# Gating the next branch during the current one, and wider buffers, in the merge of a two-layer hybrid diffusion block

## Chip, cores and metric

One Trainium2 chip, one core. The metric is the device time of one execution in microseconds, and the time of a kernel is the median of its runs. The engines in the rows below are TensorE (PE, with its weight loads as PEld), VectorE (DVE), ScalarE (ACT), GpSimd (POOL) and SyncE (SP), which issues nearly all transfers.

## The reference

Two layers work on 512 latent tokens and 256 context tokens of width 1024. A layer normalises its input, projects it to 10768 columns, and runs four mixers on slices of them: A global attention, W windowed attention, G a spatial gating MLP, and M a bidirectional mLSTM. The part that matters here joins the four:

```
y    = stack(branch_k * silu(gate_k))              # 4 branches, 512 wide each
proj = einsum('bnkw,kwd->bnkd', y, w_branch)       # each to 1024
g    = sigmoid(merge)                              # merge: 4 x 1024 of the input projection's columns
out  = sum_k(g_k * proj_k) @ w_out                 # then RMSNorm, gate, residual
```

The second layer computes its output for the latent tokens alone, so its merge runs on 512 tokens, the first layer's on 768. All data is float32.

## The kernel before

**Splitting.** Each matmul on full-precision operands is made of three: operands are split into a rounded high part (ScalarE) and a remainder (VectorE), and high x high, high x low and low x high are added in PSUM. Weights are split as they arrive (`start_load`, L206 to L228): a half is loaded to a raw buffer (pool "wr", three of them), ScalarE rounds it (L226), VectorE takes the remainder (L227).

**Stages of a layer.** Projections and mixers run interleaved (`interleave`, L1299), with results stored to device memory: branch outputs in `ydram`, gate values in `sgd`, the attentions' softmax divisors in `rsd` (L912), and, for the pairs of columns named `t...` in `FILL_ORDER` (L68), the sigmoid paths of the merge in `thd`. Then `merge` (L1346) and `finish` (L1437) run. The mLSTM is the last mixer; its head 3 runs into the beginning of the merge.

**The merge.** Branches come in the order A, W, M, G (0, 1, 3, 2). For each branch the gated product is built in four steps (L1356 to L1369): a step loads 128 channels of the branch's output and its gate, and for the two attentions the divisors, spread over 64 partitions each (L1364); VectorE multiplies (L1366, L1367), ScalarE rounds the product to `gh` (L1368), VectorE writes the remainder to `gl` (L1369). Then come eight columns of 128 outputs. A column either loads its saved sigmoid path (L1380) or computes it with 24 matmuls per 512 tokens (L1386, L1387), multiplies `gh` and `gl` by the branch's weights with 12 matmuls per 512 tokens, and adds the product of both to its running sum `zb[j]` (L1394 or L1403, L1406). The first `LEAD[l]` columns of the first branch use one-bank PSUM tiles ("d", three of them), a tile per 512 or 256 tokens; the others a two-bank tile ("s", two of them). During the last branch the finished sums are split for the output projection (`split_z`, L1431), the last two after the loop.

**Buffers.** Four SBUF pools matter: "big", 4 buffers of 12 KB per partition; "m", 8 of 3 KB; "v", 2 of 6 KB; and the weights'. Layer 1 before: the sums 0 to 3 lie in two "v" buffers, 4 to 7 in one "big"; `gh` and `gl` take two "big" buffers. The loads of a gating step and the saved sigmoid paths are all in "m". Attention values and the spatial branch's rows use "v" earlier in the layer.

**Order.** The kernel is written in a tile framework: each operation gets its priority from its place in the program, buffers are handed out in that order, and the framework fixes each engine's instruction order ahead of time by a simulated timeline. At run time every engine and SyncE's queue work strictly in that order. `stream` and `take` (L177 to L240) fix the order of the weights, one unit ahead. In layer 0 the units of the spatial branch are placed into the merge at four spots (`SPOTS`, L73); in layer 1 there are none. The prologue (L357 to L480) has an order written out by hand; its lines 473 and 474 place the split of the second weight unit.

Of the kernel before, what the change touches and what calls it, by code (L numbers as in the profile page):

```python
# [10 lines left out]
F32R = mybir.dt.float32r  # L11
# [10 lines left out]
NTOK = 768  # L22
SEQ = 512
# [32 lines left out]
MERGE0 = 6672  # L56

OFF = 250
RATIO = ((1.5, 1.3, 1.5), (1.2, 0.4, 1.5))
N2, N3 = 1, 1  # L60
LEAD = (2,4)
LAG = 26.0
SIDE_UNITS = ([(0, i) for i in range(8, 12)] + [(1, i) for i in range(8)], [(1, i) for i in range(8, 12)])
SIDE_FROM = (30, 10)
# [16 lines left out]
def tile_hybrid_block(ctx, tc, A, out):  # L81
    nc = tc.nc
    sy, act, dve, pool, pe = nc.sync, nc.scalar, nc.vector, nc.gpsimd, nc.tensor
# [23 lines left out]
    def BIG(shape, dt=F32):  # L107
        return bigp.tile(shape, dt, tag="big", name="big")

    def M(n=768, dt=F32):  # L110
        return mp.tile([128, n], dt, tag="m", name="m")

    def V6(shape, dt=F32):
        return vp.tile(shape, dt, tag="v", name="v")
# [22 lines left out]
    def bc(ap, shape):  # L137
        return ap.to_broadcast(shape)

    def rd(ap):  # L140
        return ap.bitcast(F32)
# [34 lines left out]
    BRANCHES = (0, 1, 3, 2)  # L176
# [138 lines left out]
    def load_gates(l, i):  # L315
        if i % 2 == 0:
            g = gate_g[l, i // 2] = M(512)
            sy.dma_start(out=g, in_=bc(gates[l][0:1, i * 256:i * 256 + 512], [128, 512]))
        if l == 0:
            gate_c[i] = XS()  # L320
            sy.dma_start(out=gate_c[i], in_=bc(gates[l][1:2, i * 256:i * 256 + 256], [128, 256]))
# [35 lines left out]
    def prologue():  # L357
# [69 lines left out]
        with tc.manual_schedule(engines={mybir.EngineType.PE, mybir.EngineType.Activation, mybir.EngineType.DVE, mybir.EngineType.SP}):  # L427
            wm = [load_mod(0)]
            for i in range(2):
                xx.append(BIG([128, 3, D]))  # L430
                for t in range(3 * i, 3 * i + 3):
                    sy.dma_start(out=xa(t), in_=A["x"][t] if t < XT else A["ctx"][t - XT])
            split0 = start_load(0)
            wm += [load_mod(i) for i in range(1, 4)]
            pm += [B()]
            sums_of(0)
            done = []
            jk = V6([128, D])
            r = squares(0)
            wm += [load_mod(i) for i in range(4, KT)]  # L440
            split1 = start_load(1)
            for t in range(NT):
                done.append(turned(t, r))
                if t + 1 < NT:
                    r = squares(t + 1)
                if t == 0:
                    rows_of(0)
                if t > 0:
                    back(t - 1, done[t - 1])
            column(0)  # L450
            warm(4)
            split0((0,))
            back(NT - 1, done[NT - 1])
            wh, wl = take(("in", 0, "a_kv"), 0)
            w = held["w"] = v3(wh[:, :8 * 272], 8), v3(wl[:, :8 * 272], 8)
            s2, s3 = S(), S()
            acc = [DB(), DB(), DB(), s2[:, 0:512], s2[:, 512:1024]]
            pm += [s3[:, 0:512], s3[:, 512:1024]]
            sums_of(1)
            channels(0)  # L460
            rows_of(1)
            warm(2)
            column(1)
            warm(4)
            split0((1,))
            for j in range(KT):
                if j + 1 < KT:
                    channels(j + 1)
                for i, (ps, t) in enumerate(zip(acc, TILES)):
                    if i == 2 and j + 2 < KT:  # L470
                        sums_of(j + 2)
                        rows_of(j + 2)
                    if i == 2 and j in (5, 6):
                        split1((j - 5,))
                    if i == 4 and j + 2 < KT:
                        column(j + 2)
                    tok_step(ps, w, 272, t, j)
# [868 lines left out]
    def merge(l, ydram, rsd, sgd, thd):  # L1346
        want_c = l == 0
        n = NTOK if want_c else SEQ
# [3 lines left out]
        zb = []  # L1352
        zs = {}
        done = False
        for bi, b in enumerate(BRANCHES):
            gh, gl = BIG([128, 4, NTOK], F32R), BIG([128, 4, NTOK], F32R)  # L1356
            for k in range(4):
                yt, sg = M(768), M(768)
                sy.dma_start(out=yt[:, :n], in_=ydram[b, k][:, :n])
                sy.dma_start(out=sg[:, :n], in_=sgd[b, k][:, :n])  # L1360
                if b < 2:
                    rs = M(768)
                    for i in range(2):
                        sy.dma_start(out=rs[64 * i:64 * i + 64, :n],  # L1364
                                     in_=bc(rsd[b, 2 * k + i:2 * k + i + 1, :], [64, n]))
                    dve.tensor_mul(sg[:, :n], sg[:, :n], rs[:, :n])  # L1366
                dve.tensor_mul(yt[:, :n], yt[:, :n], sg[:, :n])  # L1367
                act.copy(gh[:, k, :n], yt[:, :n])  # L1368
                dve.tensor_sub(gl[:, k, :n], yt[:, :n], rd(gh[:, k, :n]))  # L1369
            for j in range(KT):  # L1370
                if bi == 0 and j in (0, 2, 4):
                    zt = V6([128, 2, NTOK]) if j < 4 else BIG([128, 4, NTOK])
                    zb += [zt[:, i, :] for i in range(2 if j < 4 else 4)]
                z = zb[j]
# [29 lines left out]
                                             op0=ALU.add, op1=ALU.mult)  # L1404
                if bi > 0:
                    dve.tensor_add(z[:, :n], z[:, :n], th[:, :n])  # L1406
                if bi == 3 and j < 6:
                    if j == 0:
                        pt = BIG([128, 4, NTOK], F32R)
                        parts = [pt[:, i, :] for i in range(4)]  # L1410
                    elif j in (2, 4):
                        pt = V6([128, 2, NTOK], F32R)
                        parts = [pt[:, i, :] for i in range(2)]
                    elif j > 1:
                        parts = [M(768, F32R), M(768, F32R)]
                    zs[j] = split_z(z, parts, n)
                if bi == 3 and j >= 4:
                    load_gates(l, j - 4)
                if (bi, j) in SPOTS[l]:
                    while next(gating) is not None:  # L1420
                        pass
                    done = SPOTS[l][bi, j] == "g_u1"
                elif done and tails:
                    tails.pop(0)()
        pt = BIG([128, 4, NTOK], F32R)
        parts = [pt[:, i, :] for i in range(4)]
        for j in (6, 7):
            zs[j] = split_z(zb[j], parts, n)
        return zs

    def split_z(z, parts, n):  # L1431
        h, lo = parts.pop(0), parts.pop(0)
        act.copy(h[:, :n], z[:, :n])
        dve.tensor_sub(lo[:, :n], z[:, :n], rd(h[:, :n]))
        return h, lo
# [91 lines left out]
    for l in range(2):  # L1527
        ydram = dp.tile([4, 4, 128, NTOK], F32, name=f"yd{l}")
        sgd = dp.tile([4, 4, 128, NTOK], F32, name=f"sg{l}")
# [113 lines left out]
```

## Time and profile before

| | |
|---|---|
| runs | 2050.71, 2052.67, 2054.06 us; median 2052.67 |
| profiled execution | 2052.57 us, span 2050.8 us |
| mean granted TensorE clock | 0.993 of full |
| busy: PE / DVE / ACT / POOL | 97% / 64% / 47% / 4% |
| merge of layer 0 (first to last column's work) | about 850 to 1127 us of the span |
| merge of layer 1 | about 1851 to 2000 us of the span |

Busy times are of the whole span, which is made of stages with different limits; a stage is read by its own windows and by what its engines waited for. The clock column of a window is the mean of the granted TensorE clock, 1.00 for 2.4 GHz and 0.50 for 1.2 GHz. Matmul lines carry the number of the helper that issues them (L243), so they are told apart by their tiles: "d" and "s" are the PSUM tiles, "big" the gated product. A transfer's line is that of its issue on SyncE; the time to landing is listed by form.

### The profile page before, as it was taken

The page shows a single profiled execution, that of the slowest core. Times are in us where ns is not written, and L with a number is a line of the kernel's source. Part 1 is how long each engine was busy: PE and PEld are TensorE (multiplying, and loading weights), DVE is VectorE, ACT ScalarE, POOL GpSimd, SP SyncE. Part 2 cuts the span into 40 slices and gives each one's busy share as a digit, 9 for nine tenths or more (in the row PEclk, how much of TensorE's full clock was granted, in tenths as well). Part 3 has the DMA queues.
Part 4 walks back from the last instruction along what each step waited for, and adds up shares of the span by engine and source line. Part 5 has one row for each costly group of instructions (what it writes and reads, how often), then busy time and mean ns, then how long its engine had stood idle before and what let it go on. Part 6 is the DMA issues. An engine that isn't in the chain of part 4 may idle for free.

```text
span 2050.8 us, 34563 instructions
## 1 busy us (share of the span) xinstructions
PE 1992.4 (97%) x13216; PEld 1809.7 (88%) x13216; DVE 1316.1 (64%) x2857; ACT 972.9 (47%) x2178; POOL 75.1 (4%) x88
## 2 busy tenths in 40 slices
PE   7999999999999999899999989999999999998998
PEld 6898999899999899799988989989989898887778
DVE  5766865676656756567545588666685565545765
ACT  5655544354444553334332476555565465432333
POOL 1200100000000000001000021000000000000000
PEclk9999999999999999999999999999999999999999
DMA  7112223323333544665343342223333334547745
GB/s 292 63 55 78 93 94 114 122 94 126 116 106 111 181 140 152 207 217 168 100 151 115 130 153 93 84 82 111 119 117 113 124 104 160 156 136 224 239 144 180
DMA packets 124270, 274.96 MB, mean 134 GB/s; under 512 B 16032, under 2 KB 41288, under 8 KB 123464
## 3 DMA queue, kind: packets, MB, share of 16 engines
q1 hardware_dynamic: 123560, 272.13, 40.8%
q8 instruction: 104, 1.70, 0.4%
q14 instruction: 62, 0.51, 0.1%
q0 software_dynamic: 256, 0.54, 0.1%
q10 hardware_dynamic: 288, 0.07, 0.0%
HBM read 219.33 MB, written 53.36 MB: 133 GB/s over the span
## 4 chain that ended last, share of the span: by engine, by line
PE 85%; DMA 6%; DVE 4%; ACT 2%; issue 1%; SPq 0%; POOL 0%; DVEq 0%; ACTq 0%; POOLq 0%
PE d L243 59%; PE s L243 13%; PE b L243 7%; PE s L857 4%; DMA m<-rs 3%; DMA m<-sg 1%; PE d L576 1%; DVE m L1367 1%; ACT m L417 0%; DVE wl L227 0%; DMA big<-in_x_dram 0%; DMA sg<-st 0%; ACT wh L226 0%; DMA wr<-in_w_mod_dram 0%; DVE m L1366 0%
## 5 line engine op out<-in xcount | busy, mean ns | idle before, releaser
L243 PE MATMUL d<-xh,wh 128*128 128x512 f32 (+1 forms) x1504 | 537.1, 357 | 0.3 <-DVE yx L821 0.2
L243 PE MATMUL d<-xh,wl 128*128 128x512 f32 (+1 forms) x1504 | 535.1, 356 | 0.0
L243 PE MATMUL d<-xl,wh 128*128 128x512 f32 (+1 forms) x1504 | 533.2, 355 | 0.0
L227 DVE TENSOR_TENSOR wl<-wr,wh 128x1024 fp32r<-128x1024 f32 (+3 forms) x264 | 282.6, 1092 | 62.4 <-ACT wh L226 62.0
L226 ACT CAST wh<-wr 128x1024 fp32r<-128x1024 f32 (+3 forms) x264 | 238.4, 946 | 168.1 <-PE s L243 80.4
L243 PEld LDWEIGHTS d<-xh,wh 128*128 128x128 f32 x1504 | 284.5, 189 | 34.7 <-DVE st L685 0.3
L243 PEld LDWEIGHTS d<-xl,wh 128*128 128x128 f32 x1504 | 284.6, 189 | 34.3
L243 PEld LDWEIGHTS d<-xh,wl 128*128 128x128 f32 x1504 | 284.2, 189 | 34.6
L243 PE MATMUL d<-wh,xh 128*128 128x256 f32 (+1 forms) x976 | 282.6, 291 | 4.0 <-DVE xh L419 1.8
L243 PE MATMUL d<-wh,xl 128*128 128x256 f32 (+1 forms) x976 | 278.1, 285 | 0.6 <-DVE xl L420 0.5
L243 PE MATMUL d<-wl,xh 128*128 128x256 f32 (+1 forms) x976 | 278.1, 285 | 0.3 <-DVE wl L227 0.3
L243 PEld LDWEIGHTS d<-wh,xh 128*128 128x128 f32 x976 | 186.5, 192 | 7.9 <-issue 4.1
L243 PE MATMUL s<-big,wh 128*128 128x512 f32 x704 | 180.7, 363 | 8.0 <-DVE big L1369 6.5
L243 PEld LDWEIGHTS d<-wh,xl 128*128 128x128 f32 x976 | 186.9, 192 | 1.2 <-DVE xl L420 0.7
L243 PEld LDWEIGHTS d<-wl,xh 128*128 128x128 f32 x976 | 187.1, 192 | 0.8 <-DVE wl L227 0.5
L861 DVE TENSOR_TENSOR m<-s,m 128x768 fp32r<-128x768 f32 (+2 forms) x144 | 119.3, 837 | 94.9 <-ACT m L860 94.3
L825 ACT ACTIVATE m<-s,yx 128x768 f32<-128x768 f32 (+3 forms) x160 | 120.4, 753 | 97.7 <-DVE yx L823 47.8
L243 PEld LDWEIGHTS s<-big,wh 128*128 128x128 f32 x704 | 118.4, 193 | 30.6 <-DVE big L1369 7.7
L819 DVE TENSOR_REDUCE yx<-s 128x1 f32<-128x768 f32 (+3 forms) x160 | 122.5, 765 | 33.6 <-PE s L243 32.4
L860 ACT CAST m<-s 128x768 fp32r<-128x768 f32 (+2 forms) x144 | 100.7, 705 | 85.6 <-PE s L857 84.5
L243 PE MATMUL b<-m,v 128*128 128x256 f32 (+1 forms) x768 | 131.4, 285 | 0.9 <-ACT m L860 0.9
L243 PE MATMUL s<-big 128*128 128x256 f32 (+2 forms) x680 | 118.7, 303 | 1.2 <-ACT big L577 0.7
(340 smaller groups left out, 3056.1 us busy)
## 6 DMA issues: line engine op xcount, KB each, us to landing
wr<-in_w_in_dram SPq DMA_DIRECT2D x100, 512.0 KB, 4.4
wr<-in_w_mg_dram SPq DMA_DIRECT2D x50, 512.0 KB, 4.3
wr<-in_w_mod_dram SPq DMA_DIRECT2D x32, 512.0 KB, 4.5
wr<-in_w_out_dram SPq DMA_DIRECT2D x32, 512.0 KB, 4.4
th<-st SPq DMA_DIRECT2D x50, 256.0 KB, 2.3
wr<-in_w_bp_dram SPq DMA_DIRECT2D x50, 256.0 KB, 3.6
wr<-in_w_br_dram SPq DMA_DIRECT2D x28, 384.0 KB, 3.6
m<-th SPq DMA_DIRECT2D x26, 384.0 KB, 5.1
```

Source lines behind the costliest of these rows:

```text
L226: act.copy(wh[:, sl], raw)
L227: dve.tensor_sub(wl[:, sl], raw, rd(wh[:, sl]))
L243: pe.matmul(o, l, r, start=start, stop=stop)
L576: pe.transpose(pt[:, h * 128:(h + 1) * 128], st[:, h * 128:(h + 1) * 128].bitcast(F32R), ident_r)
L819: dve.reduce_max(out=mx, in_=ps[:, :n], axis=AX.X)
L825: act.activation(P, ps[:, :n], AF.Exp, bias=nm[:, 0:1], scale=sc, accum_out=sm)
L857: pe.transpose(pt[:, o:o + 128], P[:, cols[j]:cols[j] + 128], ident)
L860: act.copy(ph, pt[:, :n])
L861: dve.tensor_sub(pl, pt[:, :n], rd(ph))
L1367: dve.tensor_mul(yt[:, :n], yt[:, :n], sg[:, :n])
```

## The change

- The divisors of the first branch are no longer loaded into an "m" buffer per step, but for two steps at once into a "v" buffer, two of them.
- In layer 1 the running sums lie three to a "v" buffer (0 to 2, 3 to 5), and 6 and 7 in one "m" buffer each; none is in "big" any more.
- In layer 1 the gating steps of the next branch are written behind the columns 3 to 6 of the current one (`PP_FROM`), into a second pair of "big" buffers.
- In layer 1 the split sums lie in two "big" buffers, three sums each, and two "v" buffers for sums 6 and 7, whose split is now inside the loop. They lay in one "big", two "v" and four "m" buffers, and another "big" after the loop.
- `LEAD` goes from 2 and 4 to 4 and 6: two more columns of the first branch in one-bank tiles.
- In the prologue the first half of the second weight unit is split at input block 4 instead of 5.

```
--- before.py
+++ after.py
@@ -56,9 +56,10 @@
 MERGE0 = 6672
 
 OFF = 250
+PP_FROM = 3
 RATIO = ((1.5, 1.3, 1.5), (1.2, 0.4, 1.5))
 N2, N3 = 1, 1
-LEAD = (2,4)
+LEAD = (4,6)
 LAG = 26.0
 SIDE_UNITS = ([(0, i) for i in range(8, 12)] + [(1, i) for i in range(8)], [(1, i) for i in range(8, 12)])
 SIDE_FROM = (30, 10)
@@ -470,8 +471,8 @@
                     if i == 2 and j + 2 < KT:
                         sums_of(j + 2)
                         rows_of(j + 2)
-                    if i == 2 and j in (5, 6):
-                        split1((j - 5,))
+                    if i == 2 and j in (4, 6):
+                        split1((j // 2 - 2,))
                     if i == 4 and j + 2 < KT:
                         column(j + 2)
                     tok_step(ps, w, 272, t, j)
@@ -1352,23 +1353,53 @@
         zb = []
         zs = {}
         done = False
+        rss = {}
+
+        def gate_pair():
+            return BIG([128, 4, NTOK], F32R), BIG([128, 4, NTOK], F32R)
+
+        def load_rs(rs, b, k):
+            for i in range(2):
+                sy.dma_start(out=rs[64 * i:64 * i + 64, :n], in_=bc(rsd[b, 2 * k + i:2 * k + i + 1, :], [64, n]))
+
+        def gated(b, k, pair):
+
+            gh, gl = pair
+            if b == BRANCHES[0] and k % 2 == 0:
+                wide = V6([128, 2, NTOK])
+                for i in range(2):
+                    rss[k + i] = wide[:, i, :]
+                    load_rs(wide[:, i, :], b, k + i)
+            yt, sg = M(768), M(768)
+            sy.dma_start(out=yt[:, :n], in_=ydram[b, k][:, :n])
+            sy.dma_start(out=sg[:, :n], in_=sgd[b, k][:, :n])
+            if b < 2:
+                if b == BRANCHES[0]:
+                    rs = rss[k]
+                else:
+                    rs = M(768)
+                    load_rs(rs, b, k)
+                dve.tensor_mul(sg[:, :n], sg[:, :n], rs[:, :n])
+            dve.tensor_mul(yt[:, :n], yt[:, :n], sg[:, :n])
+            act.copy(gh[:, k, :n], yt[:, :n])
+            dve.tensor_sub(gl[:, k, :n], yt[:, :n], rd(gh[:, k, :n]))
+
+        nxt = None
         for bi, b in enumerate(BRANCHES):
-            gh, gl = BIG([128, 4, NTOK], F32R), BIG([128, 4, NTOK], F32R)
-            for k in range(4):
-                yt, sg = M(768), M(768)
-                sy.dma_start(out=yt[:, :n], in_=ydram[b, k][:, :n])
-                sy.dma_start(out=sg[:, :n], in_=sgd[b, k][:, :n])
-                if b < 2:
-                    rs = M(768)
-                    for i in range(2):
-                        sy.dma_start(out=rs[64 * i:64 * i + 64, :n],
-                                     in_=bc(rsd[b, 2 * k + i:2 * k + i + 1, :], [64, n]))
-                    dve.tensor_mul(sg[:, :n], sg[:, :n], rs[:, :n])
-                dve.tensor_mul(yt[:, :n], yt[:, :n], sg[:, :n])
-                act.copy(gh[:, k, :n], yt[:, :n])
-                dve.tensor_sub(gl[:, k, :n], yt[:, :n], rd(gh[:, k, :n]))
+            if nxt is None:
+                nxt = gate_pair()
+                for k in range(4):
+                    gated(b, k, nxt)
+            gh, gl = nxt
+            nxt = None
             for j in range(KT):
-                if bi == 0 and j in (0, 2, 4):
+                if bi == 0 and not want_c and j in (0, 3, 6, 7):
+                    if j < 6:
+                        zt = V6([128, 3, SEQ])
+                        zb += [zt[:, i, :] for i in range(3)]
+                    else:
+                        zb.append(M(768))
+                elif bi == 0 and want_c and j in (0, 2, 4):
                     zt = V6([128, 2, NTOK]) if j < 4 else BIG([128, 4, NTOK])
                     zb += [zt[:, i, :] for i in range(2 if j < 4 else 4)]
                 z = zb[j]
@@ -1404,7 +1435,17 @@
                                              op0=ALU.add, op1=ALU.mult)
                 if bi > 0:
                     dve.tensor_add(z[:, :n], z[:, :n], th[:, :n])
-                if bi == 3 and j < 6:
+                if bi == 3 and not want_c:
+                    if j in (0, 3):
+                        pt = BIG([128, 6, SEQ], F32R)
+                        parts = [pt[:, i, :] for i in range(6)]
+                    elif j == 6:
+                        pt = V6([128, 3, SEQ], F32R)
+                        parts = [pt[:, i, :] for i in range(3)]
+                    elif j == 7:
+                        parts.append(V6([128, 3, SEQ], F32R)[:, 0, :])
+                    zs[j] = split_z(z, parts, n)
+                elif bi == 3 and j < 6:
                     if j == 0:
                         pt = BIG([128, 4, NTOK], F32R)
                         parts = [pt[:, i, :] for i in range(4)]
@@ -1416,16 +1457,21 @@
                     zs[j] = split_z(z, parts, n)
                 if bi == 3 and j >= 4:
                     load_gates(l, j - 4)
+                if not want_c and bi < 3 and j >= PP_FROM and j < PP_FROM + 4:
+                    if nxt is None:
+                        nxt = gate_pair()
+                    gated(BRANCHES[bi + 1], j - PP_FROM, nxt)
                 if (bi, j) in SPOTS[l]:
                     while next(gating) is not None:
                         pass
                     done = SPOTS[l][bi, j] == "g_u1"
                 elif done and tails:
                     tails.pop(0)()
-        pt = BIG([128, 4, NTOK], F32R)
-        parts = [pt[:, i, :] for i in range(4)]
-        for j in (6, 7):
-            zs[j] = split_z(zb[j], parts, n)
+        if want_c:
+            pt = BIG([128, 4, NTOK], F32R)
+            parts = [pt[:, i, :] for i in range(4)]
+            for j in (6, 7):
+                zs[j] = split_z(zb[j], parts, n)
         return zs
 
     def split_z(z, parts, n):
```

## Rows read from the trace of the kernel before

**Rows 1.** The page, busy time, share of the span and instructions of each engine
```profile
PE 1992.4 (97%) x13216; PEld 1809.7 (88%) x13216; DVE 1316.1 (64%) x2857; ACT 972.9 (47%) x2178; POOL 75.1 (4%) x88
```

**Rows 2.** Who TensorE waited for, 840 to 870 us: total, times, longest
```profile
PE d L243 <- ACT big L1368: 7.2, 2, 5.2
```

**Rows 3.** The same view, 1840 to 2005 us
```profile
PE s L243 <- DVE big L1369: 4.5, 2, 2.6
PE d L243 <- ACT big L1368: 3.4, 3, 1.7
PE d L243 <- ACT wh L226: 1.7, 1, 1.7
PE s L243 <- DVE m L1403: 0.3, 1, 0.3
```

**Rows 4.** Windows: length, each engine's busy time, PE clock, DMA share, GB/s
```profile
860.00:870.00 10.00, 8.34 (x35) 7.08 (x36) 5.10 (x13) 1.00 (x2) 1.32 (x1) 0.66 0.81 254
```

**Rows 5.** The same view, in layer 1's merge
```profile
1910.00:1920.00 10.00, 10.00 (x46) 8.26 (x45) 7.87 (x13) 3.53 (x6) 0.00 (x0) 1.00 0.95 335
1920.00:1930.00 10.00, 8.17 (x29) 6.30 (x28) 7.76 (x13) 2.38 (x4) 0.00 (x0) 0.83 0.81 270
1910.00:1950.00 40.00, 37.26 (x154) 29.46 (x152) 30.17 (x48) 12.28 (x21) 0.00 (x0) 0.96 0.81 268
```

**Rows 6.** Timeline of SyncE, layer 0: start us, us, engine, line, transfer, count
```profile
811.67 0.32 SPq L1359 DMA_DIRECT2D m<-yd  x1
...
821.37 0.32 SPq L1360 DMA_DIRECT2D m<-sg  x1
...
829.51 1.16 SPq L1364 DMA_DIRECT2D m<-rs  x2
...
852.09 1.09 SPq L1364 DMA_DIRECT2D m<-rs  x2
...
870.66 0.33 SPq L1148 DMA_DIRECT2D yd<-m  x1
```

**Rows 7.** Timeline of VectorE, layer 0 (idle before and releaser in brackets)
```profile
833.61 0.96 DVE L1366 TENSOR_TENSOR m<-m 128x768 f32<-128x768 f32 x1 [1.08 <-DMA m<-rs]
834.60 0.96 DVE L1367 TENSOR_TENSOR m<-m 128x768 f32<-128x768 f32 x1
...
858.79 0.96 DVE L1366 TENSOR_TENSOR m<-m 128x768 f32<-128x768 f32 x1 [3.32 <-DMA m<-rs]
...
861.64 0.96 DVE L1369 TENSOR_TENSOR big<-m,big 128x768 fp32r<-128x768 f32 x1 [0.81 <-ACT big L1368]
```

**Rows 8.** By line, first and last start: divisor stores, layer 1's softmax, spatial stores
```profile
L912 SPq DMA_DIRECT2D rs<-xs x4: 318/331/416, 396.9 to 1729.1; - x4
...
L825 ACT ACTIVATE m<-s,yx x64: 672/850/927, 1254.3 to 1707.4; 128x768 f32<-128x768 f32 x32, 128x512 f32<-128x512 f32 x16, 128x640 f32<-128x640 f32 x16
...
L760 SPq DMA_DIRECT2D yd<-t x8: 360/371/384, 1656.8 to 1687.8; - x8
```

**Rows 9.** Transfers by form: count, KB of one, median us to landing
```profile
m<-sg SPq DMA_DIRECT2D x16, 384.0 KB, 5.2
...
m<-sg SPq DMA_DIRECT2D x16, 256.0 KB, 3.6
...
m<-th SPq DMA_DIRECT2D x24, 256.0 KB, 3.5
...
wr<-in_w_bp_dram SPq DMA_DIRECT2D x50, 256.0 KB, 3.6
```

**Rows 10.** Chain that ended last, 1900 to 1925 us: start, us, what
```profile
1904.05 7.96 PE s L243 x35
```

**Rows 11.** Timeline of VectorE, end of layer 1's second branch
```profile
1923.58 0.69 DVE L1367 TENSOR_TENSOR m<-m 128x512 f32<-128x512 f32 x1 [1.29 <-DMA m<-sg]
1924.19 1.89 DVE L1369 TENSOR_TENSOR big<-m,big 128x512 fp32r<-128x512 f32 x3
```

**Rows 12.** Timeline of SyncE, layer 1: store of the last mLSTM head
```profile
1879.82 0.49 SPq L1148 DMA_DIRECT2D yd<-m  x1
```

## Prediction

> **What bounds the kernel now.** I read the busy times first: TensorE is busy for 97% of the span [rows 1], so only time in which it stands still, or runs at half clock, can be won without taking matmuls away, and the change takes none away. Next, the list of who waited for whom on TensorE, limited to the two merges. In layer 0's merge TensorE waited 7.2 us in two pieces for ScalarE's rounding of the first branch's gated product (L1368) [rows 2]. In layer 1's merge it waited 4.5 us for the remainder of the gated product (L1369), 3.4 us for L1368, 1.7 us for a weight rounding (L226) and 0.3 us for an evacuation [rows 3]. Then the 10-us windows, for the clock. After each long stop it falls from 2.4 to 1.2 GHz: a mean of 0.66 means that (1 - 0.66) / 0.5 = 0.68 of the window, 6.8 us, ran at half rate [rows 4]; 0.83 means 3.4 us, in the window from 1920 and again in that from 1950 [rows 5]. Half rate costs half of the time in which TensorE had work.
>
> Last, the SyncE queue, for why the gated products are late. In layer 0 a value tile is requested at 811.67, its gate tile at 821.37, its divisor tile at 829.51, and the fourth divisor at 852.09 [rows 6]. All are buffers of the pool "m". That pool has 8, and I count 5 held by the last mLSTM head (two key products, the value tile, the output-gate tile and the tile that becomes its result), which is stored only at 870.66. So one step's three tiles use all three free buffers, and the next step starts when they come back: VectorE multiplies by the first divisor at 833.61 and by the fourth at 858.79, (858.79 - 833.61) / 3 = 8.4 us a step [rows 7].
>
> **The change, part by part.**
>
> *Divisors in two wide buffers.* The third tile of each of the four steps leaves pool "m". Its two transfers can go as soon as the pool "v" has room and the divisors are stored. The four stores of divisors lie between 396.9 and 1729.1, two per layer; layer 1's last softmax, which ends the use of the attention's values, starts at 1707.4, and the spatial branch, the third user of "v" there, stores its last piece at 1687.8 [rows 8]. In both layers that is long before the divisors are wanted, so I cost their loads at nothing; SyncE's spare time hides them, and without that cover they cost what they cost now. The third free "m" buffer then holds the next step's value tile. A step becomes: gate tile's load 5.2 us in layer 0 [rows 9], then two products, after which its buffer is free. The products are 1 us each (from 833.61 to 834.60 [rows 7]), so a step is 5.2 + 2 = 7.2 us if only one gate tile is in flight. The first product no longer waits for the divisor requested at 829.51 but for the gate tile requested at 821.37 [rows 6]: 821.4 + 5.2 + 3 x 7.2 + 3 (two products, rounding and remainder) is about 852, where the last remainder starts now at 861.64 [rows 7]. That removes about 10 us of lateness against 7.2 us of waiting [rows 2]: I take all 7.2. With the stop goes the half clock: 6.8 us [rows 4], of which TensorE stood still for about 1.7 (10 - 8.34 busy), so (6.8 - 1.7) / 2 = 2.6. Term A: -9.8 us (0 if the buffers, not the divisors, set the pace). What is late next is the first column's evacuation, which needs its saved gate tile; I let the three small banks cover that.
>
> In layer 1 the same chain accounts for 3.4 us, and the 1.7 us on L226 follow from it, since that weight buffer comes free only when the delayed first column ends [rows 3]. Term B: -5.1 us (bounds 0 and -5.1).
>
> *Sums packed 3+3+2, next branch gated during the current one (layer 1).* One "big" buffer comes free, so two pairs of gated products fit, and the remainder no longer waits for the last matmul of the branch before. That is the 4.5 us, in two pieces before branches 3 and 2, and the 0.3 behind the first; two stretches at half clock follow, 3.4 / 2 = 1.7 us each [rows 3, 5]. Together 8.2 us. What limits the gain: from column 3 of branch 1 to the end of branch 3 there are 13 columns of 12 matmuls; 35 take 7.96 us [rows 10], so a column is 2.73 and TensorE needs 35.5 us. VectorE: 26 sums and products, 14 weight remainders, 16 gating operations, 56 at 0.60 us back to back (three take 1.89, the last ends 0.69 after its start) [rows 11], 33.6 us: just under. DMA: 13 saved gate tiles, 14 half weight loads and 16 gating tiles of 256 KB [rows 9], 43 x 0.262 = 11.3 MB; in 35.5 us that is 318 GB/s. The best 10 us here moved 335 at a DMA share of 0.95, the 40 us around it 268 at 0.81 [rows 5]. I take 290, between these, since prefetching in the long columns before helps: 39.1 us, so 3.6 us is given back. Term C: -4.6 us (bounds 0, if 268 stays the rate, and -8.2).
>
> The Trainium skill (DMA: Bandwidth & Descriptors, Specifications) gives about 358 GB/s as one core's limit towards HBM. By it 11.3 MB take 31.6 us, TensorE would hide them, and the sum would be 3.6 us lower; no window read here reached that rate.
>
> *Split of the last sums inside the loop.* Work of the same size, moved before two columns; "out" matmuls now follow without a stop, so 0. *More columns in single banks.* Same matmuls; two smaller evacuations instead of one in layer 0, beside TensorE: 0. *Prologue.* One weight split one step earlier: 0, bounds -0.5 and +0.5.
>
> *New waits.* In layer 1 sums 6 and 7 now hold two "m" buffers until the last branch, and the next branch's gating loads are requested ahead of later columns' saved gate tiles. In the first branch, while the mLSTM head still holds its five buffers (its store waits until 1879.82 [rows 12]), a column may wait for a buffer. Nothing here shows it; bounds 0 and one 3.5 us landing [rows 9] per column for four columns, 14. I take +2, nearer to nothing, because the gated products come earlier and the head frees its buffers in that very stretch. Term D: +2.
>
> Sum: -9.8 - 5.1 - 4.6 + 2 = -17.5. The profiled execution took 2052.57 us (span 2050.8 and 1.8 around it), 0.1 from the median 2052.67 of the runs. 2052.6 - 17.5 = 2035.1: I forecast **2035**.
>
> **Rivals.**
> 1. *The DMA engines keep up*: C is whole, 2035.1 - 3.6 = 2031.5. For it: a share of 0.95 was reached once; against it: only once.
> 2. *The transitions gain nothing*: VectorE or DMA is late instead, C is 0 and D stands at 2 to 6: 2039.7 to 2044. For it: VectorE's 33.6 us against 35.5 leaves 5%.
> 3. *Buffers, not divisors, set the first branch's pace*: A and B are 0, C and D stay: 2050.0; if the gate tile's load is hidden for half, 2045. For it: gate tiles too are requested only as buffers return.
> 4. *The planner orders it as before*: the instruction order follows a simulated timeline, and priorities shift it little; then about 2052.6.
> 5. *Slower: saved gate tiles starve in pool "m" in layer 1.* With six buffers left, a column at which a gating step is issued waits for that step: load 3.6 [rows 9], product, rounding and remainder 0.6 to 0.7 each [rows 11], 5.6 us in place of 2.73, 2.9 more. With 4 columns in each of three branches: +35, so 2070; at half of them 2052.6. It decides once two steps' tiles and a column's own don't fit in six buffers (2 x 2 + 1 = 5 for branches 3 and 2, so just not; 2 x 3 + 1 = 7 for branch 1). For it: today all eight serve these loads. Against it: today four value tiles lie waiting at each transition, which ends.
>
> **How the numbers follow.** Chances: forecast 0.42 (its own range 2033 to 2038), rival 1 0.20, rival 2 0.14, rival 3 0.07, rival 4 0.05, rival 5 0.12. The range runs from 2027 (rival 1 without D, and some slack at the first branch) to 2048, which takes in rival 2 and the milder part of rival 3 and leaves out about 0.2. A measurement tells 0.2%, 4 us, from no change: faster 0.82, same 0.06, slower 0.12.
>
> **What would show it.** In the profile after: no wait of TensorE on L1368 above 1 us in either merge and no half clock at the start of layer 0's merge (A, B); divisor loads into "v" far ahead of the merge; remainders of branches 3 and 2 computed before the last column of the branch before, DMA share about 0.9 there (C). Wrong would be: waits of the same length under another name (L1394 or L1403 on saved gate tiles, loads of "m" late), which is rival 2 or 5, or gating steps still 8 us apart, rival 3.

## The result and the profile after

The changed kernel took 2027.45 us (median of 4 runs, 2026.75 to 2029.01) beside 2052.66 us for the kernel before (4 runs): a ratio of 0.9889, 95% interval 0.9875 to 0.9902, so 25.2 us less. I had forecast 17.5 less, 2035 in a range from 2027 to 2048, so the result lies half a us inside the range's lower end. The profiled execution took 2029.01 us, its span is 2027.2.

TensorE has less idle time, and about 8 us less busy time for the same matmuls [rows 1], since fewer of them ran at half clock (1.2 GHz in place of 2.4). The page of the changed kernel, busy time, share and instructions:

```profile
PE 1983.9 (98%) x13216; PEld 1805.3 (89%) x13216; DVE 1314.6 (65%) x2859; ACT 972.7 (48%) x2178; POOL 77.9 (4%) x88
```

**Where the time went.** A landmark that both programs have is the store of the mLSTM's factors, once per layer (L1025 before, L1026 after). It cuts the span into a start (all before the first store), a middle (layer 0's mLSTM and merge, its output projection, the start of layer 1) and an end (layer 1's mLSTM, merge and output). That line in the kernel before, then in the changed one; "421.2 to 1499.0" are the first and last start:

```profile
L1025 SPq DMA_DIRECT2D nmd<-gca x4: 707/742/877, 422.3 to 1510.5; - x4
```

```profile
L1026 SPq DMA_DIRECT2D nmd<-gca x4: 723/750/853, 421.2 to 1499.0; - x4
```

Start: 422.3 to 421.2, 1.1 less. Middle: 1088.2 to 1077.8, 10.4 less. End (to the end of the span): 540.3 to 528.2, 12.1 less. Together 23.6, the difference of the two spans.

**Layer 0's merge.** Nothing is left of the 7.2 us of waiting [rows 2]: between 800 and 880 us the list of TensorE's waits is empty. The windows (length, busy time of each engine, granted clock, DMA share, GB/s) show it busy throughout, at 2.4 GHz, where one before stood at 0.66 [rows 4]:

```profile
850.00:860.00 10.00, 10.00 (x61) 8.86 (x60) 6.20 (x19) 3.07 (x15) 1.32 (x1) 1.00 0.85 279
860.00:870.00 10.00, 10.00 (x64) 8.93 (x63) 3.36 (x5) 1.84 (x3) 0.00 (x0) 1.00 0.94 316
```

The cause stands in VectorE's timeline (columns as in [rows 7]; L1382 multiplies by the divisor, now in "v", L1383 is the second product, L1385 the remainder):

```profile
822.61 0.96 DVE L1382 TENSOR_TENSOR m<-m,v 128x768 f32<-128x768 f32 x1 [0.31 <-DMA m<-sg]
...
830.07 0.96 DVE L1382 TENSOR_TENSOR m<-m,v 128x768 f32<-128x768 f32 x1 [1.34 <-DMA m<-sg]
...
835.58 0.96 DVE L1382 TENSOR_TENSOR m<-m,v 128x768 f32<-128x768 f32 x1 [1.70 <-DMA m<-sg]
836.58 0.96 DVE L1383 TENSOR_TENSOR m<-m 128x768 f32<-128x768 f32 x1
...
841.04 0.96 DVE L1382 TENSOR_TENSOR m<-m,v 128x768 f32<-128x768 f32 x1 [1.39 <-DMA m<-sg]
...
844.17 0.96 DVE L1385 TENSOR_TENSOR big<-m,big 128x768 fp32r<-128x768 f32 x1 [0.18 <-ACT big L1384]
```

The first product starts at 822.6 instead of 833.6, a step takes (841.04 - 822.61) / 3 = 6.1 us instead of 8.4, and the last remainder starts at 844.2 instead of 861.6. VectorE's short waits are for the gate tile now. SyncE requests the third and fourth gate tile here:

```profile
832.05 0.32 SPq L1375 DMA_DIRECT2D m<-sg  x1
...
837.56 0.32 SPq L1375 DMA_DIRECT2D m<-sg  x1
```

The fourth is requested as the second product of the step before ends (836.58 + 0.96), and its own first product starts 3.5 us later. So one gate tile is in flight at a time, and each of the last two steps is its landing and two products, 5.5 us (the first took 7.5). The divisors themselves were loaded long before (form, count, issue times, first and last start):

```profile
L1363 SPq DMA_DIRECT2D v<-rs x16: 450/586/677, 400.2 to 1716.1; - x16
```

**Layer 1's merge.** TensorE's waits from 1840 to 2005 us (line waited for, total, times, longest); compare [rows 3], which leaves out two lines of its view, 0.2 us on L1368 and this one:

```profile
PE s L243 <- DVE big L1403: 0.6, 1, 0.6
```

The changed kernel's whole list:

```profile
PE s L244 <- ACT big L1384: 2.6, 4, 1.0
PE s L244 <- DVE m L1434: 0.7, 1, 0.7
```

With these two lines it was 10.7 us of waits; it has become 3.3, all from 1901 to 1924 us, around the two transitions, none in the first branch, and no window of the merge has a clock below 1.00 [rows 5]:

```profile
1900.00:1910.00 10.00, 9.05 (x40) 6.84 (x39) 9.50 (x16) 2.38 (x4) 0.00 (x0) 1.00 0.92 296
1910.00:1920.00 10.00, 8.79 (x38) 6.68 (x36) 6.01 (x10) 3.31 (x6) 0.00 (x0) 1.00 0.69 220
1920.00:1930.00 10.00, 8.87 (x38) 7.11 (x39) 9.93 (x17) 3.05 (x6) 0.00 (x0) 1.00 0.89 291
```

TensorE is short of work by about a tenth there, in pieces of up to 1.0 us.

### The profile page after: what moved, and what is told of

It is laid out like the page before. It is cut to its first block, busy times and chain, and to the rows that moved or that the text cites. A ratio compares the mean times of both kernels' runs of the same rounds, so it can differ in the third digit from the quotient of the medians.

```text
span 2027.2 us, 34553 instructions
## 1 busy us (share of the span) xinstructions
PE 1983.9 (98%) x13216; PEld 1805.3 (89%) x13216; DVE 1314.6 (65%) x2859; ACT 972.7 (48%) x2178; POOL 77.9 (4%) x88
## 5 line engine op out<-in xcount | busy, mean ns | idle before, releaser
L244 PE MATMUL s<-big,wh 128*128 128x512 f32 (+1 forms) x656 | 163.8, 357 | 6.1 <-ACT big L1384 2.6
L244 PEld LDWEIGHTS s<-big,wh 128*128 128x128 f32 x656 | 107.3, 188 | 26.1 <-ACT big L1384 4.7
```

What stands on the lines that cost most here:

```text
L244: pe.matmul(o, l, r, start=start, stop=stop)
```

## The experiments

My theory: the divisors in "v" (terms A and B) and the early gating (term C) give what was won, each about as forecast. The rivals: one part gives it all, or the time went by another way (the longer lead, the prologue, buffers rather than divisors). All runs in one table. The times are medians; "profiled" is the execution that the stretches (those above) are read from. In brackets behind a stretch: the time in which TensorE did nothing, and what half clock cost it (its busy time multiplied by 1 minus the granted clock), both added up from windows of 1 us.

| kernel | runs | us | ratio to before (interval) | profiled | middle | end |
|---|---|---|---|---|---|---|
| before | 4 | 2052.66 | 1 | 2052.57 | 1088.2 (18.4, 5.9) | 540.3 (24.1, 5.0) |
| changed | 4 | 2027.45 | 0.9889 (0.9875 to 0.9902) | 2029.01 | 1077.8 (11.2, 3.4) | 528.2 (16.3, 1.5) |
| 1 divisors back in "m" | 6 | 2042.45 | 0.9955 (0.9941 to 0.9968) | 2047.72 | 1089.3 (17.7, 7.9) | 535.6 (20.3, 5.1) |
| 2 no early gating | 6 | 2037.07 | 0.9926 (0.9913 to 0.9938) | 2037.47 | 1076.4 (10.0, 3.3) | 537.5 (20.0, 5.9) |
| 3 lead as before | 5 | 2028.74 | 0.9890 (0.9875 to 0.9906) | 2027.57 | 1077.6 (12.1, 1.7) | 527.2 (14.6, 3.0) |
| 4 prologue as before | 5 | 2028.87 | 0.9884 (0.9868 to 0.9899) | 2024.37 | 1073.8 (9.3, 1.6) | 527.7 (16.0, 1.7) |
| 5 before + wide divisors | 5 | 2035.87 | 0.9931 (0.9918 to 0.9944) | 2036.66 | 1083.4 (14.3, 6.5) | 530.6 (17.9, 3.4) |
| 6 before + wide values | 7 | 2043.10 | 0.9961 (0.9945 to 0.9976) | 2046.22 | 1085.8 (16.2, 6.0) | 536.7 (20.0, 6.5) |
| 7 gating a column earlier | 4 | 2027.75 | 0.9892 (0.9877 to 0.9908) | 2029.59 | 1079.8 (11.7, 4.8) | 527.4 (14.2, 3.1) |
| 8 two "m" buffers taken out | 4 | 2027.99 | 0.9894 (0.9876 to 0.9912) | 2026.58 | 1077.1 (10.2, 3.4) | 526.6 (15.5, 1.5) |
| 9 before + wide divisors + lead | 6 | 2032.86 | 0.9910 (0.9895 to 0.9926) | 2033.11 | 1076.5 (10.1, 3.4) | 532.4 (18.1, 5.1) |
| 10 spatial stores on ScalarE | 4 | 2027.31 | 0.9876 (0.9857 to 0.9895) | 2027.78 | 1077.6 (9.7, 5.1) | 527.4 (15.6, 1.7) |

The kernel before, run beside them on the same chips, took 2053.44 us (numbers 1 to 4), 2050.21 (5 to 8) and 2051.95 (9 and 10). What is left of a stretch without its brackets is nearly the same in all twelve, 1062.6 to 1063.9 us in the middle and 509.2 to 511.6 in the end, so the brackets tell where the time went. Two cautions. The stretches are those of one execution each: that of numbers 1 and 6 was their slowest, 5.3 and 3.1 us above the median, that of number 4 its fastest, 4.5 below. And half clock comes in pieces that cost up to 1.7 us each and that one execution has and another not (last section): number 4 differs from the changed kernel by an edit in the prologue alone, and its middle is 4.0 shorter, 1.9 of it standing still and 1.8 one such piece. What is less than that tells nothing there. The end is steadier: 526.6 to 528.2 over the six kernels with wide divisors and early gating.

### 1. The divisors back in pool "m"

```
-            if b == BRANCHES[0] and k % 2 == 0:
-                wide = V6([128, 2, NTOK])
...
-                if b == BRANCHES[0]:
-                    rs = rss[k]
-                else:
-                    rs = M(768)
-                    load_rs(rs, b, k)
+                rs = M(768)
+                load_rs(rs, b, k)
```

> The changed kernel with the first branch's divisors back in one buffer of pool m per step. Theory: the third m buffer and the divisors' place in the chain set the pace of the first branch's gating, so a step in layer 0 is 8 to 9 us again (6.1 with the change), TensorE waits some 7 us in layer 0 and 3 to 5 us in layer 1 for the gated product, with a stretch at half clock in layer 0: 2027.5 + 12 to 18 = 2039 to 2045 us. Rival (the early gating or the single banks carry the gain, and the divisors were hidden anyway): under 2031 us.

Measured: 2042.45, 15.0 us above the changed kernel, and the old wait is back. TensorE's waits from 800 to 880 us:

```profile
PE d L244 <- ACT big L1376: 6.5, 2, 4.1
PE s L244 <- ACT m L1129: 0.5, 1, 0.5
```

Middle and end of the profiled execution, the slowest of six, are longer by 11.5 and 7.4. In layer 1 TensorE waits 1.9 us for the gated product again, less than the 3 to 5 that I expected, 1.7 for a weight remainder, and 2.6 for a scaling in the mLSTM (L1129), for which it waits there in neither of the two kernels. By the medians the divisors are worth about 15 us on top of the rest, as A + B had it (14.9).

### 2. The early gating left out

```
-PP_FROM = 3
+PP_FROM = 8
```

The next branch is then gated at its own start, as before; the packed sums and the second pair of buffers stay.

> The changed kernel with each branch gated at its own start in layer 1 again, the sums still packed 3+3+2, so that two pairs of gated products still fit. Theory: it is the second pair of big buffers that matters, the planner moves the gating forward by itself: 1 to 3 us slower, 2028.5 to 2030.5, no half clock. Rival (the place in the program decides): the two stops before branches 3 and 2 are back with two stretches at half clock, 5 to 8 us slower, 2032 to 2035.

Measured: 2037.07, 9.6 us above the changed kernel and above both ranges that I gave; the end stretch is 9.3 longer. Spare buffers alone win nothing here; the place of the gating in the program does. TensorE's waits from 1840 to 2005 us, and a window with the clock behind one of them:

```profile
PE s L244 <- DVE m L1434: 3.6, 4, 1.7
PE s L244 <- ACT big L1384: 2.2, 2, 2.0
PE s L244 <- DVE big L1385: 1.0, 1, 1.0
```

```profile
1880.00:1890.00 10.00, 6.99 (x24) 4.85 (x23) 4.66 (x7) 2.65 (x5) 0.00 (x0) 0.78 0.62 197
```

The loss is larger than term C (4.6): TensorE stands still 3.7 us longer in the end stretch, and half clock costs 4.4 more. Number 9, which has neither packing nor early gating, is 5.1 shorter in that stretch, but the intervals of the two ratios overlap. So that packing without early gating is worse than neither is not shown. Two sums in "m" would be the obvious suspect, but number 8 takes two more buffers away and loses nothing.

### 3 and 4. The lead and the prologue as before

```
-LEAD = (4,6)
+LEAD = (2,4)
```

> The changed kernel with 2 and 4 columns of the first branch in single banks, as before. Theory: nothing, 2027.5 within 2 us, since TensorE stood still there for the gated product, not for a PSUM tile. Rival (with the gated product early, TensorE meets the two-bank tiles while the last mLSTM head still uses them): a wait of TensorE on L1434 or on the head's evacuations of 2 to 6 us in the first branch, 2030 to 2034.

Measured: 2028.74, inside the noise of the changed kernel. Yet a wait is there that the changed kernel lacks, before the last transpose of the mLSTM head, which comes next on TensorE once the two small-bank columns are done:

```profile
PE s L1147 <- DVE m L1141: 2.8, 1, 2.8
```

The middle is no longer for it: another stop, near 1207 us (L577), lasts 1.1 us there and 3.9 in the changed kernel, and there is one piece of half clock less (1.7 in place of 3.4). So by this run the lead removes a wait and wins nothing measurable. Number 9 says otherwise, below.

```
-                    if i == 2 and j in (4, 6):
-                        split1((j // 2 - 2,))
+                    if i == 2 and j in (5, 6):
+                        split1((j - 5,))
```

> The changed kernel with the prologue's split at input blocks 5 and 6 again. Theory: the split at block 5 delays the last two rounded inputs, TensorE stops for 1.8 us instead of 0.7 near 53 us of the span and falls to half clock for 3.4 us after it: 1 to 2.5 us slower, 2028.5 to 2030, with the first half-clock stretch of the kernel before back at about 55 us. Rival (the early stop was an accident of that execution): 2027.5 within 0.7 us.

Measured: 2028.87, inside the noise of the changed kernel. In the profiled execution, the fastest of five, the stop of 1.8 us in the prologue, 0.7 in the changed kernel, is back, but not the half clock that followed it in the kernel before. TensorE's waits from 40 to 70 us here, then the window from 50 us, in the kernel before and here:

```profile
PE d L244 <- DVE xh L420: 1.8, 1, 1.8
```

```profile
50.00:60.00 10.00, 7.72 (x48) 7.27 (x48) 9.06 (x33) 5.49 (x16) 2.12 (x3) 0.83 0.34 108
```

```profile
50.00:60.00 10.00, 7.69 (x59) 7.03 (x58) 9.07 (x32) 6.02 (x18) 2.12 (x3) 1.00 0.32 108
```

The first store at 422.3 before and 421.1 here (421.2 in the changed kernel) shows that the 1.1 us of the start stretch belong to that half clock and not to the stop itself. Whether the edit makes the half clock rarer is open: with the old order two of five profiled executions had it (the kernel before and number 6), with the new order none of seven.

### 5. Only the wide divisors, in the kernel before

```
+                if bi == 0 and k % 2 == 0:
+                    wide = V6([128, 2, NTOK])
...
-                    rs = M(768)
+                    if bi == 0:
+                        rs = wide[:, k % 2, :]
+                    else:
+                        rs = M(768)
...
```

> The kernel before with the divisors of the first branch in two wide buffers of pool v, in both layers, and nothing else of the change. Theory: terms A and B alone, 9.8 and 5.1 us, and a stretch at half clock or two less: 2053.4 - 15 to 19 = 2034 to 2038 us; the 4.5 us of waits before branches 3 and 2 of layer 1 stay. Rival (the divisors help only together with the early gating, since without it the time is lost again at the next branch): 2042 to 2048.

Measured: 2035.87 beside 2050.21, 14.3 less: A + B was 14.9. The transitions of layer 1 keep their waits, as they should (TensorE, 1840 to 2005 us):

```profile
PE s L243 <- DVE big L1378: 4.2, 2, 2.3
PE s L243 <- DVE m L1412: 0.3, 1, 0.3
PE s L243 <- ACT big L1377: 0.2, 1, 0.2
```

In layer 0 a new one of 2.8 us takes the place of the old 7.2 (800 to 880 us): the mLSTM's last transpose again, with two first columns in small banks.

```profile
PE s L1146 <- DVE m L1140: 2.8, 1, 2.8
```

### 6. Only the value tiles wide, in the kernel before

Here a buffer of "m" comes free per step as in number 5, but the divisor stays the tile that is loaded last.

```
+                if bi == 0 and k % 2 == 0:
+                    wide = V6([128, 2, NTOK])
+                    for kk in range(2):
+                        sy.dma_start(out=wide[:, kk, :n], in_=ydram[b, k + kk][:, :n])
+                if bi == 0:
+                    yt, sg = wide[:, k % 2, :], M(768)
...
```

> The kernel before with the first branch's value tiles, instead of its divisors, loaded ahead into two wide buffers of pool v; the divisors stay in pool m, requested last. Theory, buffers: a step needs two m buffers instead of three whichever tile has left, so the same as with the divisors out, 2034 to 2038 us, steps of 6 to 7 us in layer 0. Rival, order of arrival: the divisors come last in a step, so a step is shorter only where they have left; with them still in the chain steps stay near 8 us and the time within 3 us of before, 2050 to 2053.

Measured: 2043.10 beside 2050.21, 7.1 less, half of number 5 and between the two ranges that I gave. One of its seven runs took 2034.38; its granted clock was 0.997, that of the other six 0.992 to 0.994. VectorE's timeline (L1373 multiplies by the divisor, L1110 is the mLSTM's state):

```profile
824.50 0.96 DVE L1373 TENSOR_TENSOR m<-m 128x768 f32<-128x768 f32 x1 [1.74 <-DMA m<-rs]
...
843.85 0.96 DVE L1373 TENSOR_TENSOR m<-m 128x768 f32<-128x768 f32 x1 [1.06 <-DMA m<-rs]
844.73 0.34 DVE L1110 SCALAR_TENSOR_TENSOR xs<-xs,gaa,b 128x129 f32<-128x129 f32 x1
```

(843.85 - 824.50) / 3 = 6.45 us a step: nearly all of the faster pace comes from the free buffer, whichever tile leaves "m". But VectorE works in order, and the mLSTM's small operations stand behind the products. It stands 7.2 us before the four first products here, 4.7 in the changed kernel, and the last remainder starts at 846.9, 2.7 later. TensorE waits for those operations instead (800 to 880 us):

```profile
PE b L243 <- DVE xs L1110: 3.7, 1, 3.7
PE s L1146 <- DVE m L1140: 2.3, 1, 2.3
```

So my step "the divisors set the pace" was half right: the buffer sets the pace. That the early divisor wins the rest by keeping VectorE free for others is in part argued. Of the 9.5 us by which the profiled execution is longer than number 5's, 4.1 are standing still, half of them in the end stretch, which I have not followed, and 4.3 are half clock, which is partly chance.

### 7 and 8. Earlier gating, and fewer buffers

```
-PP_FROM = 3
+PP_FROM = 2
```

> The changed kernel with the next branch's gating steps written behind columns 2 to 5 instead of 3 to 6 in layer 1. Theory: the 2.6 us of short waits on L1384 at the beginning of branches 3 and 2, where the last two steps come late, shrink to under 1 us, 2025.5 to 2027. Rival (buffers of pool m, handed out in the order of the program, are the limit): the saved gate tiles of columns 3 to 5 come later instead, 2028 to 2033.

```
+            if not want_c and bi == 1:
+                spare = [M(768) for _ in range(2)]
+                for s in spare:
+                    dve.memset(s[:, 0:8], 0.0)
...
+                if not want_c and bi == 3 and j == 7:
+                    for s in spare:
+                        dve.memset(s[:, 0:8], 0.0)
```

> The changed kernel with two buffers of pool m taken out of use in layer 1 from its second branch on (allocated, 8 columns of each set to zero, so four are left for loads). Theory: a gating step and the next saved gate tile fit in four, just; loads start later, TensorE waits 3 to 8 us more: 2030 to 2036. Rival 5 of the prediction, starvation: each of 12 columns waits for a gating step, 2.9 us each: 2050 to 2065. Rival, DMA or VectorE is what limits the stretch and buffers are idle: within 1.5 us of 2027.5.

Measured: 2027.75 and 2027.99, both as the changed kernel; I had expected 2025.5 to 2027 and 2030 to 2036. With the gating a column earlier the waits on the rounding (L1384) fall from 2.6 us to 0.2 (TensorE, 1865 to 2005 us), and the end stretch is 0.8 shorter, less than can be told from nothing. TensorE stands still 2.1 us less in it, but half clock costs 1.6 more, behind two stops near 1672 us that both kernels have, ahead of the merge. The list:

```profile
PE s L244 <- DVE m L1434: 0.8, 1, 0.8
PE s L244 <- ACT wh L227: 0.5, 1, 0.5
PE s L244 <- ACT big L1384: 0.2, 1, 0.2
PE s L244 <- DVE big L1385: 0.2, 1, 0.2
```

With four instead of six "m" buffers for layer 1's last three branches the end stretch is 526.6, 1.6 shorter rather than longer. Starved saved gate tiles, my rival 5, are not there. Term D was about the first branch, which this edit leaves alone; there the changed kernel's own list has no wait at all.

### 9. Wide divisors and the longer lead, in the kernel before

The edit of number 5, and

```
-LEAD = (2,4)
+LEAD = (4,6)
```

> The kernel before with the first branch's divisors in two wide buffers in both layers and four instead of two first columns of layer 0 in one-bank tiles; the layer-1 packing and early gating stay out. Theory (the longer lead is worth something once the divisors are early): the wait of 2.8 us before the mLSTM's last transpose at 857 us in layer 0 and the half clock behind it (3.4 us, worth 1.7) go, so 2.8 to 4.5 us less than with the divisors alone: 2031 to 2033.5. What is then left to the change (2027.5) is what the early gating of layer 1 is worth, 3.5 to 6 us. Rival (the lead is worth nothing, as I forecast; what TensorE does not wait for there it waits for at the next branch): 2035 to 2037, as with the divisors alone, and the early gating is worth 8 us.

Measured: 2032.86 beside 2051.95, 19.1 less, 4.8 more than number 5 by the two differences, though the intervals of the two ratios overlap. The wait before the transpose is gone: TensorE's list from 800 to 880 us is empty, and the middle is 6.9 shorter, 4.2 of it standing still and 3.1 half clock. What the changed kernel has beyond this one is the early gating with its packing (and the prologue): 2032.86 - 2027.45 = 5.4 us in the medians, 4.2 in the end stretch. The transitions still wait here:

```profile
PE s L243 <- DVE big L1378: 4.2, 2, 2.4
PE s L243 <- DVE m L1412: 0.5, 2, 0.3
PE s L243 <- ACT big L1377: 0.3, 1, 0.3
```

### 10. An attempt at more: the spatial stores on another queue

The longest stop left in the changed kernel's merges is 2.3 us on L1385 at 1062 us, before layer 0's last branch. SyncE stood before a store of the spatial branch with the gating loads behind it (its waits from 1040 to 1060 us):

```profile
SPq L761 <- ACT t L760: 8.0, 1, 8.0
```

```
-        sy.dma_start(out=dst.rearrange("g p t -> p g t"), in_=v3(ys, 2))
+        act.dma_start(out=dst.rearrange("g p t -> p g t"), in_=v3(ys, 2))
```

> The changed kernel with the stores of the spatial branch's results issued by ScalarE's queue instead of SyncE's. In the changed kernel's layer 0 SyncE stands 9.5 us before such a store (1043 to 1052 us) with the third and fourth gating step's loads of the last branch behind it, and no transfer runs for most of that time; TensorE then waits 2.3 us for the third remainder at 1062 us. Theory (the store in SyncE's queue makes the loads late): the 2.3 us go, and in executions in which half clock follows that stop another 1.7: 2024 to 2025.5. Rival (the loads would wait for buffers of pool m in any case, or ScalarE's issuing of sixteen stores delays its evacuations as much): 2027 to 2029.

Measured: 2027.31, no gain. The next entry of the queue, a weight load that waits for its buffer, holds the loads as long (the same view):

```profile
SPq L213 <- DVE wl L228: 8.5, 2, 8.4
```

The stop stays, 2.1 us. Neither the theory nor the rival as I wrote it: the loads waited neither for the store alone nor for "m", but for whatever stands ahead of them in SyncE's order.

## Why the prediction was right, and where its sizes were off

**Term A (-9.8).** Right in place, cause and size: the wait on L1368 and its half clock went, because the first branch's tiles no longer fill "m". In the middle stretch TensorE stands still 7.2 us less, and half clock costs 2.5 less. Inside the term the step was mis-sized: I had 7.2 us a step and the last remainder at about 852 (my own addends give 851), and it is 6.1 and 844.2. One gate tile is in flight at a time, as I had it, but it lands 3.0 to 3.5 us after its request, not 5.2, the median over all tiles of this form. This did not show in the term, which could win no more than the wait. Number 6 mends the reason: rival 3 (the buffers, not the divisors, set the pace) was right on the pace, but wrong on the result, since freeing the divisor's buffer is itself what the change does.

**Term B (-5.1).** Right by the waits: the 5.1 that I counted [rows 3] are gone, and 0.6 on L1403 with them. The runs that isolate it show more. The end stretch fell from 540.3 to 530.6 and 532.4 with wide divisors and without early gating (numbers 5 and 9), 9.7 and 7.9. TensorE stands still 6.2 and 6.0 less in them; half clock costs 1.6 less in number 5 (one transition's piece did not come, though its wait stayed) and 0.1 more in number 9. Some 2 us in each are neither, and stay open.

**Term C (-4.6).** Right: 4.2 us in the end stretch and 5.4 in the medians between number 9 and the changed kernel. The end stretch of number 1, which has the early gating without the wide divisors, is 4.7 below that of the kernel before, in the slowest of its executions. Most of it is half clock, as forecast: between number 9 and the changed kernel 3.6 us of half clock went and 1.8 of standing still; the sum had 3.4, and 1.2 (4.8 less the 3.6 given back). (The give-back is 3.4 by its own figures: 11.3 MB at 290 GB/s take 38.9 us, not 39.1. And at 268 they take 42.1, which leaves 1.6 of gain, not the bound 0.) One sign that I had named was not met: the last two remainders of the third branch start at 1902.6 and 1905.2, while that branch's first column already waits for its product. What limited the gain was forecast as DMA at 290 GB/s over the whole stretch. The windows moved 296, 220 and 291, with VectorE at 9.5 and 9.9 us of 10 in the outer two, so the transfers were not the one limit. The Trainium skill (DMA: Bandwidth & Descriptors, Specifications) gives about 358 GB/s as one core's limit towards HBM. The trace does not bear that out as a limit: while the first weights and inputs were loaded, the kernel before moved 417 GB/s.

```profile
10.00:20.00 10.00, 7.94 (x40) 6.50 (x40) 6.86 (x10) 7.54 (x16) 4.44 (x10) 1.00 1.03 417
```

For the gain it did not decide: all half clock of the two transitions went although 3.3 us of waiting stayed.

**Term D (+2).** Wrong: 0. The first branch has no wait in the changed kernel's list, and taking two more buffers away from the later branches (number 8) cost nothing.

**The parts at nothing.** Prologue: nothing that can be told from the noise (number 4). Split inside the loop: no wait of the output's first matmuls on it is in the profile after. The lead: the sum had 0, and the runs leave it between 0 (number 3) and about 5 us (number 9 against 5). What I overlooked is that it covers the mLSTM's last transpose: once the divisors are early, TensorE has nothing else to do in order before that transpose.

**The sum, and luck.** By stretches: start -1.1, middle -10.4 against A's -9.8, end -12.1 against B + C + D's -7.7. By kind: of the 23.6 us between the spans 15.0 are standing still, where the sum had 11.5, and 7.7 are half clock, where it had 6.0. The 6.1 us between forecast and span are then 3.5 of standing still, 2.0 of them term D, 1.7 of half clock, and 0.9 that are neither. The half clock that I had counted, at the first branch of layer 0 and at the two transitions, cost 6.1 before and is gone. Other pieces came and went and cancel out. The 1.7 on top are the prologue's piece, which the kernel before had in its profiled execution and three other kernels with the same order did not: that part is luck, as far as these runs tell.

**Rival 1** (2031.5) was nearer than the forecast, but not by its own reason: 3.3 us of waiting stayed at the transitions. **Rivals 2, 4 and 5** fell: the transitions gained, the order changed, and nothing starved.

## What to carry to other kernels

When a step's loads fill a pool, ask which tile can be loaded into another pool long before: the buffer it frees sets the pace of the rest (number 6), and an engine that works in order may stand less before it with other work behind. A second pair of buffers is worth nothing until the program asks for the next stage early, since loads and buffers are handed out in program order (number 2). And a blocked queue is not cured by removing the entry at its head: look what stands second (number 10).

## What the runs showed of the hardware that I had not expected

I wrote that after each long stop the clock falls to 1.2 GHz. It does not after each. A stop of 1.8 us on the same line, in the prologue, was followed by half clock in one kernel (0.83 from 50 to 60 us) and not in another (1.00), as shown under number 4. The stop of 2.1 us before layer 0's last branch in number 10 was followed by it, that of 2.3 us in the changed kernel was not (number 10, then the changed kernel):

```profile
1060.00:1070.00 10.00, 9.59 (x46) 8.23 (x46) 7.18 (x10) 1.24 (x3) 0.00 (x0) 0.83 0.63 203
```

```profile
1060.00:1070.00 10.00, 7.85 (x44) 6.75 (x45) 8.32 (x11) 2.03 (x3) 0.00 (x0) 1.00 0.76 258
```

The same holds for the stop of 2.8 us before the mLSTM's last transpose: half clock behind it in number 5 (0.91 and 0.92 from 850 to 870 us), none in number 3 (1.00). None of the stops of up to 1.0 us in the changed kernel's transitions was followed by it. So a stop of some 2 us carries a chance of 1.7 us more (half of 3.4), not a certainty, and that is part of the 2 to 12 us by which executions of one kernel differ. In number 6, where they differ by 11.8, the granted clocks of the slowest and the fastest, 0.992 and 0.997, account for some 10 by my estimate (0.005 of 2040). Number 9 waits 5.0 us at the transitions, in stops of up to 2.4, and has two pieces of half clock; the changed kernel waits 3.3, in stops of up to 1.0, and has none. Splitting the stops took the half clock away here although two thirds of the waiting stayed.
